# First layer's modulation on TensorE in quarters of its columns, with the norm's sums and products on VectorE

## The chip, the cores and the metric

The kernel runs on one core of a Trainium2 chip. What counts is the device time of one execution in microseconds (us). Below, a DMA is a transfer between the chip's main memory and the on-chip memory, a chunk is 128 rows of a weight matrix, and a record is one line of the profiler for one instruction on an engine.

## What is computed

Two transformer-like blocks stand one behind the other: a two-layer joint attention block with a modulation by a conditioning vector, then a block with a state-space mixer, latent attention and a gated feed-forward net. All of it is float32. The change touches the beginning of layer 0 of the first block only:

```python
silu_c = jax.nn.silu(c)            # one vector of 2048 for the 256 latent tokens
silu_cc = jax.nn.silu(c_ctx)       # one for the 256 context tokens
shift, scale, gate = jnp.split(silu_c @ w_mod[l] + b_mod[l], 3, axis=-1)
shift_c, scale_c, gate_c = jnp.split(silu_cc @ w_mod[l] + b_mod[l], 3, axis=-1)
n = rms_norm(h, pre_norm_g[l]) * (1.0 + scale[:, None]) + shift[:, None]
nc = rms_norm(hc, pre_norm_g[l]) * (1.0 + scale_c) + shift_c
p = jnp.split(n @ w_in[l], split_points, axis=-1)
```

`w_mod[0]` has 2048 rows and 6144 columns. Before the first product with `w_in` can be taken, the 4096 columns of shift and scale must have been multiplied with the two vectors.

## The kernel before

Activations lie with the 2048 features on partitions, as 16 chunks of 128 features by 512 tokens (256 latent, 256 context) in `hb`. The norm is taken in three steps: sums of squares over the features (`first_norm`, lines 824 to 843), the row `rb` of reciprocal roots (`rstd_row`), and the product of `hb` with `rb` (`times_rb`, lines 793 to 796). `norm_in` (line 784) then applies scale and shift chunk by chunk on ScalarE and splits the result into a high part `nH` and a rest `nL`.

The modulation is taken in blocks of 512 columns. `mod_first(q, steps)` (line 696) makes block q: it loads 16 chunks of 128 rows by 512 columns (`mraw`, 256 KB each), and multiplies each by the two vectors, which stand in `cs` (128 partitions, 16 chunks, 2 vectors). The odd chunks k = 1, 3, ..., 15 go to TensorE (line 708, weights `cs[:, k, :]`, two columns, output on two partitions of the PSUM bank `S`). Chunk 0 goes to ScalarE (line 706) and the even chunks 2 to 14 to VectorE (`mod_acc`, line 666), each once for either vector, into `acc`. Two more matmuls (line 717) sum `acc` over the partitions into the same bank. ScalarE copies the two rows out (line 719), and `finish`, which is run after the first chunks of the block that follows, turns them with four transposes (line 724), adds the bias (line 725), and for q below 4 makes the gains `gsc` (line 781).

The blocks come in the order 4, 0, 5, 1, 6, 2, 7, 3. Blocks 4 and 0 give scale and shift of features 0 to 511, and so on. Beside blocks 5 to 7 and 1 to 3 runs `first_steps(j)`: it takes the weights of two column groups of `w_in` for four chunks, applies `norm_in` to these four chunks, multiplies `rb` into the next four chunks on GpSimd, and issues the first products (lines 370 to 372, 96 matmuls of 256 columns for each j). It is a generator; `mod_first` advances it by one step after each chunk from the third on, which fixes the order of the instructions on each engine. The order is by hand: every engine works through its queue in program order.

The chunks land in 22 slots that go round (`slots`, 16 chunks a block), and SyncE issues each transfer when its slot has been read. The same queue carries `raw`, the weights of `w_in`.

Of the kernel before, what the change touches and what calls it, by code (L numbers as in the profile page):

```python
# [11 lines left out]
F32 = mybir.dt.float32  # L12
F32R = mybir.dt.float32r
I32 = mybir.dt.int32
AF = mybir.ActivationFunctionType
ALU = mybir.AluOpType
AX = mybir.AxisListType
ADD, SUB, MUL, MAX = ALU.add, ALU.subtract, ALU.mult, ALU.max
# [226 lines left out]
def program(ctx: ExitStack, tc: tile.TileContext, A, stop=None):  # L245
    nc = tc.nc
    V, S, P, T, SY = nc.vector, nc.scalar, nc.gpsimd, nc.tensor, nc.sync
    ctx.enter_context(tc.manual_schedule())

    const = ctx.enter_context(tc.tile_pool(name="const", bufs=1))  # L250
# [5 lines left out]
    def cst(name, shape, src=None, eng=None):  # L256
        t = const.tile(list(shape), F32, name=name)
        if src is not None:
            (eng or S).dma_start(out=t, in_=A[src])
        return t  # L260
# [3 lines left out]
    def ps_(tag):  # L264
        return psp.tile([128, 512], F32, tag=tag, name=tag, bufs=PSB[tag])
# [254 lines left out]
    ident = cst("ident", [128, 128], "ident")  # L520
# [1 line left out]
    V.memset(ones, 1.0)  # L522
    mhalf = const.tile([128, 8], F32, name="mhalf")
    V.memset(mhalf, -0.5)
    sel = const.tile([128, 2, 2], F32, name="sel")
    V.memset(sel, 0.0)
    for v in range(2):
        V.memset(sel[:, v, v:v + 1], 1.0)
    bmod = cst("bmod", [128, 2, 48], "bmod")
    preg = cst("preg", [128, 2, 16], "preg")  # L530
    postg = cst("postg", [128, 2, 16], "postg")
# [31 lines left out]
    def rstd_row(tag, accs, n, dim, out, first=0):  # L563

        tiles, t = [], 0
        while t < n:
            w = min(128, n - t) if t or not first else first
            tiles.append((t, w))
            t += w
        pst = ps_(tag)  # L570
        for i, (t, w) in enumerate(tiles):
            for j, acc in enumerate(accs):
                T.matmul(pst[:w, i:i + 1], acc[:, t:t + w], ones[:, 0:1], start=j == 0, stop=j == len(accs) - 1)
        yield
        v, r = small("rv", 4, 1), small("rr", 4, 1)
        for w in sorted({w for _, w in tiles}):
            idx = [i for i, x in enumerate(tiles) if x[1] == w]
            c = slice(idx[0], idx[-1] + 1)
            V.tensor_scalar(v[:w, c], pst[:w, c], 1.0 / dim, EPS, op0=MUL, op1=ADD)
            P.tensor_tensor(out=r[:w, c], in0=v[:w, c], in1=mhalf[:w, c], op=ALU.pow)  # L580
        yield
        psb = ps_(tag)
        for i, (t, w) in enumerate(tiles):
            T.matmul(psb[:, t:t + w], r[:w, i:i + 1].to_broadcast([w, 128]), ident[:w, :w], start=True, stop=True)
        yield
        S.copy(out=out, in_=psb[:, :n])
# [12 lines left out]
    aw = b1.enter_context(tc.tile_pool(name="aw", bufs=2))  # L599
# [10 lines left out]
    def t2k(name="t2"):  # L610
        return aw.tile([128, 512], F32, tag="t2", name=name, bufs=3)

    def p2k(name="P"):
        return aw.tile([128, 512], F32, tag="P", name=name, bufs=3)
# [38 lines left out]
    cs = const.tile([128, 16, 2], F32, name="cs")  # L653
# [5 lines left out]
    V.scalar_tensor_tensor(out=cs, in0=thv, scalar=1.0, in1=cT, op0=ADD, op1=MUL)  # L659
    V.tensor_scalar(cs, cs, 0.5, None, op0=MUL)  # L660

    def mod_acc(acc, v, k, w, first):
        if first:
            V.tensor_scalar(acc, w, cs[:, k, v:v + 1], None, op0=MUL)
        else:
            V.scalar_tensor_tensor(out=acc, in0=w, scalar=cs[:, k, v:v + 1], in1=acc, op0=MUL, op1=ADD)  # L666
# [14 lines left out]
    def mod_load(q):  # L681

        out = [next(slot) for _ in range(16)]
        k = 0
        while k < 16:
            t, j = out[k]
            n = 1
            while k + n < 16 and n < 4 and out[k + n][0] is t:
                n += 1
            SY.dma_start(out=t[:, j:j + n, :], in_=mod_src(0, q, k, n))  # L690
            k += n
        return [t[:, j, :] for t, j in out]

    fins = []

    def mod_first(q, steps):

        raw = mod_load(q)
        ps = ps_("S")
        acc = aw.tile([128, 2, 512], F32, tag=("pth", "ptl")[q // 4], name="acc", bufs=1)  # L700
        acc = [acc[:, v, :] for v in range(2)]
        on_pe = [k for k in range(1, 16) if k not in (2,4,6,8,10,12,14)]
        for k in range(16):
            if k == 0:
                for v in range(2):
                    S.activation(out=acc[v], in_=raw[0], func=AF.Copy, scale=cs[:, 0, v:v + 1])
            elif k in on_pe:
                T.matmul(ps[:2, :], cs[:, k, :], raw[k], start=(k == on_pe[0]), stop=False)
            else:
                for v in range(2):  # L710
                    mod_acc(acc[v], v, k, raw[k], False)
            if k == 2 and fins:
                fins.pop(0)()
            elif k > 2:
                next(steps, None)
        for v in range(2):
            T.matmul(ps[:2, :], sel[:, v, :], acc[v], start=False, stop=(v == 1))
        row = aw.tile([2, 512], F32, tag="sqa", name="row", bufs=1)
        S.copy(out=row, in_=ps[:2, :])

        def finish():
            pt = ps_("X")
            for j in range(4):
                T.transpose(pt[:, 2 * j:2 * j + 2], row[:, j * 128:(j + 1) * 128], ident[:2, :2])
            V.tensor_tensor(out=mod[0][:, :, 4 * q:4 * q + 4].rearrange("p v j -> p j v"),
                            in0=pt[:, :8].rearrange("p (j v) -> p j v", v=2),
                            in1=bmod[:, 0, 4 * q:4 * q + 4].unsqueeze(2).to_broadcast([128, 4, 2]), op=ADD)
            if q < 4:
                gains(0, 4 * q, 4 * q + 4)
        fins.append(finish)  # L730

    def mod_later(l, q, vs):
# [8 lines left out]
        for k in range(16):  # L741
            w = raws.pop(k)
            for v in vs:
                mod_acc(acc[v], v, k, w, k == 0)
            if k < 14:
                raws[k + 2] = load(k + 2)
            if k % 2:
                yield
                yield
# [30 lines left out]
    def gains(l, k0, k1, vs=slice(0, 2)):  # L780
        V.scalar_tensor_tensor(out=gsc[:, vs, k0:k1], in0=mod[l][:, vs, 16 + k0:16 + k1], scalar=1.0,
                               in1=preg[:, l, k0:k1].unsqueeze(1).to_broadcast([128, vs.stop - vs.start, k1 - k0]), op0=ADD, op1=MUL)

    def norm_in(k):

        t = t2k("nrm")
        for v, c in enumerate((LATC, CTXC)):
            S.activation(out=t[:, c[0]:c[1]], in_=hb[:, k, 2 + c[0]:2 + c[1]], func=AF.Identity,
                         scale=gsc[:, v, k:k + 1], bias=mod[0][:, v, k:k + 1])
        split(nH[:, k, :], nL[:, k, :], t)  # L790
# [3 lines left out]
    def times_rb(j, eng):  # L794
        for k in range(4 * j, 4 * j + 4):
            eng.tensor_tensor(out=hb[:, k, 2:514], in0=hb[:, k, 2:514], in1=rb, op=MUL)
# [4 lines left out]
    def first_steps(j):  # L801

        ws = []
        for i in DUO:
            ws.append(W.take((0,) + WIN[i][0], 256, False))
            yield
        for k in range(4):
            norm_in(4 * j + k)
            yield
        if j < 3:  # L810
            times_rb(j + 1, P)
        for _ in range(0):
            yield
        for i in range(4):
            for ps, w, prods in zip(duo_ps, ws, map(prod_of, DUO)):
                prods(ps, w[i:i + 1], N_, (FULL, FULL), 4 * j + i, KC, lambda t, k: t[:, k, :])
                for _ in range(2):
                    yield
# [5 lines left out]
    def first_norm():  # L824
        xacc, xacc2 = p2k("xacc"), p2k("xacc2")
        for k in range(16):
            xs = hb[:, k, 2:514]
            if k < 2:
                S.activation(out=(xacc, xacc2)[k], in_=xs, func=AF.Square)
            else:  # L830
                sq = t2k("sq")
                S.activation(out=sq, in_=xs, func=AF.Square)
                if k % 3 == 1:
                    P.tensor_tensor(out=xacc2, in0=xacc2, in1=sq, op=ADD)
                else:
                    V.tensor_tensor(out=xacc, in0=xacc, in1=sq, op=ADD)
            if k % 4 == 3:
                yield
        V.tensor_tensor(out=xacc, in0=xacc, in1=xacc2, op=ADD)
        yield  # L840
        yield from rstd_row("O", [xacc], 512, D, rb)
        yield
        times_rb(0, P)

    steps = first_norm()
    for _ in range(4):
# [771 lines left out]
    def mt_(name, shape, dt=F32, src=None):  # L1618
        t = m2.tile(list(shape), dt, name=name)
        if src:  # L1620
            SY.dma_start(out=t, in_=A[src])
        return t
# [686 lines left out]
    out = mt_("out", [128, 16, 256])  # L2309
# [22 lines left out]
```

## Time and profile before

| | us |
|---|---|
| median of 3 runs (3022.82 to 3035.22) | 3023.95 |
| the profiled execution | 3022.74 |
| its span, first to last instruction | 3021.0 |
| of it up to the first gains `gsc` | 64.15 |
| from there to the second, to the third, to the fourth | 34.12, 34.10, 32.61 |
| all that follows | 2856 |

The rows further down come from the page of that one execution and from questions to its trace. PE is TensorE, PEld its weight loads, DVE VectorE, ACT ScalarE, POOL GpSimd, and SPq the queue of SyncE, from which most transfers are issued. `S`, `X`, `mm` and `PT` are PSUM banks; names in the form out<-in are those of the code.

### The profile page before, as it was taken

The page shows a single profiled execution, that of the slowest core. Times are in us where ns is not written, and L with a number is a line of the kernel's source. Part 1 is how long each engine was busy: PE and PEld are TensorE (multiplying, and loading weights), DVE is VectorE, ACT ScalarE, POOL GpSimd, SP SyncE. Part 2 cuts the span into 40 slices and gives each one's busy share as a digit, 9 for nine tenths or more (in the row PEclk, how much of TensorE's full clock was granted, in tenths as well). Part 3 has the DMA queues.
Part 4 walks back from the last instruction along what each step waited for, and adds up shares of the span by engine and source line. Part 5 has one row for each costly group of instructions (what it writes and reads, how often), then busy time and mean ns, then how long its engine had stood idle before and what let it go on. Part 6 is the DMA issues. An engine that isn't in the chain of part 4 may idle for free. (4 is left out here: it accounts for less than half of the span.)

```text
span 3021.0 us, 48873 instructions
## 1 busy us (share of the span) xinstructions
PE 2823.6 (93%) x18894; PEld 2525.3 (84%) x18894; DVE 2058.2 (68%) x3801; ACT 1289.0 (43%) x2212; POOL 553.2 (18%) x521
## 2 busy tenths in 40 slices
PE   5999999999899987999998998799899999999998
PEld 1477897897787887889898897776899999999998
DVE  6668767678677568776667887776865555455644
ACT  3335423434344344544435644234354444344443
POOL 4001100100112143010001125654531110001100
PEclk9999999999999998999999998899999999999999
DMA  8744454454445664634443464341455565665554
GB/s 306 271 129 132 129 151 129 150 155 139 118 122 157 209 188 160 199 118 139 149 142 100 145 215 140 124 128 61 145 166 176 183 182 183 185 186 184 185 175 154
DMA packets 176441, 483.96 MB, mean 160 GB/s; under 512 B 20944, under 2 KB 32848, under 8 KB 176208
## 3 DMA queue, kind: packets, MB, share of 16 engines
q1 hardware_dynamic: 171312, 468.62, 49.9%
q0 software_dynamic: 2880, 9.96, 0.9%
q8 instruction: 148, 2.42, 0.3%
q10 hardware_dynamic: 2016, 2.25, 0.2%
q14 instruction: 85, 0.70, 0.1%
HBM read 468.71 MB, written 12.06 MB: 159 GB/s over the span
## 5 line engine op out<-in xcount | busy, mean ns | idle before, releaser
L327 DVE TENSOR_TENSOR wl<-raw,wh 128x1024 fp32r<-128x1024 f32 (+2 forms) x650 | 813.5, 1256 | 441.0 <-ACT wh L313 436.3
L313 ACT CAST wh<-raw 128x1024 fp32r<-128x1024 f32 (+2 forms) x650 | 669.7, 1036 | 924.2 <-PE mm L465 571.5
L464 PE MATMUL mm<-nH,wh 128*128 128x512 f32 (+1 forms) x2048 | 705.2, 344 | 11.8 <-ACT kp L1121 6.7
L465 PE MATMUL mm<-nL,wh 128*128 128x512 f32 (+1 forms) x2048 | 697.7, 341 | 4.6 <-DVE nL L1109 4.6
L466 PE MATMUL mm<-nH,wl 128*128 128x512 f32 (+1 forms) x2048 | 696.9, 340 | 3.5 <-DVE wl L327 3.5
L464 PEld LDWEIGHTS mm<-nH,wh 128*128 128x128 f32 x2048 | 390.3, 191 | 63.8 <-ACT kp L1121 7.1
L666 DVE SCALAR_TENSOR_TENSOR acc<-mraw,cs,acc 128x512 f32<-128x512 f32 x532 | 383.5, 775 | 80.9 <-DMA mraw<-in_wmod 46.2
L465 PEld LDWEIGHTS mm<-nL,wh 128*128 128x128 f32 x2048 | 390.2, 191 | 51.1 <-DVE nL L1109 6.4
L466 PEld LDWEIGHTS mm<-nH,wl 128*128 128x128 f32 x2048 | 389.4, 190 | 51.3 <-DVE wl L327 4.3
L464 PE MATMUL mm<-ZA,wh 128*128 128x258 f32 (+1 forms) x1408 | 400.4, 284 | 5.0 <-DVE oa L1910 5.0
L466 PE MATMUL mm<-ZA,wl 128*128 128x258 f32 (+1 forms) x1408 | 399.9, 284 | 0.0
L465 PE MATMUL mm<-ZB,wh 128*128 128x258 f32 (+1 forms) x1290 | 363.9, 282 | 0.0
L464 PEld LDWEIGHTS mm<-ZA,wh 128*128 128x128 f32 x1408 | 267.3, 190 | 5.2 <-issue 5.2
L466 PEld LDWEIGHTS mm<-ZA,wl 128*128 128x128 f32 x1408 | 267.5, 190 | 0.0
L465 PEld LDWEIGHTS mm<-ZB,wh 128*128 128x128 f32 x1290 | 245.3, 190 | 0.0
L370 PE MATMUL mm<-wh,nH 128*128 128x256 f32 x736 | 212.9, 289 | 8.9 <-ACT nH L470 4.7
L372 PE MATMUL mm<-wh,nL 128*128 128x256 f32 x736 | 210.8, 286 | 5.3 <-DVE nL L471 3.8
L371 PE MATMUL mm<-wl,nH 128*128 128x256 f32 x736 | 209.8, 285 | 0.0
L464 PE MATMUL mm<-yH,wh 128*128 128x256 f32 x688 | 193.3, 281 | 0.0
L465 PE MATMUL mm<-yL,wh 128*128 128x256 f32 x688 | 193.3, 281 | 0.0
L466 PE MATMUL mm<-yH,wl 128*128 128x256 f32 x688 | 193.3, 281 | 0.0
L370 PEld LDWEIGHTS mm<-wh,nH 128*128 128x128 f32 x736 | 141.2, 192 | 30.6 <-issue 18.1
(502 smaller groups left out, 4846.1 us busy)
## 6 DMA issues: line engine op xcount, KB each, us to landing
raw<-in_win SPq DMA_DIRECT2D x266, 512.0 KB, 3.8
raw<-in_wup SPq DMA_DIRECT2D x172, 512.0 KB, 4.2
mraw<-in_wmod SPq DMA_DIRECT2D x288, 256.0 KB, 2.9
raw<-in_wout SPq DMA_DIRECT2D x76, 512.0 KB, 4.0
raw<-in_wda SPq DMA_DIRECT2D x40, 512.0 KB, 3.6
raw<-in_wdb SPq DMA_DIRECT2D x40, 512.0 KB, 4.3
mraw<-in_wmod SPq DMA_DIRECT2D x28, 512.0 KB, 5.4
mraw<-in_wmod SPq DMA_DIRECT2D x10, 1024.0 KB, 5.7
```

Source lines behind the costliest of these rows:

```text
L313: S.copy(out=h[:, :size], in_=self.raw[j][:, :size])
L327: V.tensor_sub(lo[:, :size], r[:, :size], h[:, :size].bitcast(F32))
L370: T.matmul(o, ah, w[i][0], start=(k == 0 and t % 2 == 0), stop=False)
L371: T.matmul(o, ah, w[i][1], start=False, stop=False)
L372: T.matmul(o, al, w[i][0], start=False, stop=(k == nk - 1 and t % 2 == 1 and last and i == len(w) - 1))
L464: T.matmul(out, wh, ah, start=start, stop=False)
L465: T.matmul(out, wh, al, start=False, stop=False)
L466: T.matmul(out, wl, ah, start=False, stop=stop)
L666: V.scalar_tensor_tensor(out=acc, in0=w, scalar=cs[:, k, v:v + 1], in1=acc, op0=MUL, op1=ADD)
```

## The change

The sums of all 16 chunks of a block go to TensorE. The two columns of `cs` are padded with 30 columns of zeros to 32 (`csq`), and of each four chunks the first writes partitions 0 to 31 of the bank `S`, the second 32 to 63, and so on: four matmuls in a row on four quarters of the array's columns. A block then leaves four partial sums for either vector; ScalarE copies all 128 partitions, and in `finish` four matmuls with a selector `sel` of two columns sum the quarters and turn the result at once, in place of the four transposes. The products of ScalarE and VectorE with the chunks and the two matmuls with `acc` are gone. `first_steps` is advanced by two steps after the first four chunks of a block, and by four after each further four. All sums of squares, a third of which were on GpSimd, and the products with `rb` go to VectorE.

```diff
-    sel = const.tile([128, 2, 2], F32, name="sel")
-    V.memset(sel, 0.0)
-    for v in range(2):
-        V.memset(sel[:, v, v:v + 1], 1.0)
+
+    sel = const.tile([128, 2], F32, name="sel")
+    V.tensor_reduce(out=sel, in_=ident.rearrange("p (j c) -> p c j", c=32)[:, 0:2, :], axis=AX.X, op=ADD)
...
+    csq = aw.tile([128, 16, 32], F32, tag="pth", name="csq", bufs=1)
+    V.memset(csq, 0.0)
+    V.tensor_copy(out=csq[:, :, 0:2], in_=cs)
...
         ps = ps_("S")
-        acc = aw.tile([128, 2, 512], F32, tag=("pth", "ptl")[q // 4], name="acc", bufs=1)
-        acc = [acc[:, v, :] for v in range(2)]
-        on_pe = [k for k in range(1, 16) if k not in (2,4,6,8,10,12,14)]
-        for k in range(16):
-            if k == 0:
-                for v in range(2):
-                    S.activation(out=acc[v], in_=raw[0], func=AF.Copy, scale=cs[:, 0, v:v + 1])
-            elif k in on_pe:
-                T.matmul(ps[:2, :], cs[:, k, :], raw[k], start=(k == on_pe[0]), stop=False)
-            else:
-                for v in range(2):
-                    mod_acc(acc[v], v, k, raw[k], False)
-            if k == 2 and fins:
+        for k0 in range(0, 16, 4):
+
+            for j in range(4):
+                T.matmul(ps[32 * j:32 * j + 32, :], csq[:, k0 + j, :], raw[k0 + j], start=(k0 == 0), stop=(k0 == 12))
+            if k0 == 0 and fins:
                 fins.pop(0)()
-            elif k > 2:
+            for _ in range(2 if k0 == 0 else 4):
                 next(steps, None)
-        for v in range(2):
-            T.matmul(ps[:2, :], sel[:, v, :], acc[v], start=False, stop=(v == 1))
-        row = aw.tile([2, 512], F32, tag="sqa", name="row", bufs=1)
-        S.copy(out=row, in_=ps[:2, :])
+        row = aw.tile([128, 512], F32, tag=("sqa", "ptl")[q // 4], name="row", bufs=1)
+        S.copy(out=row, in_=ps)
...
-                T.transpose(pt[:, 2 * j:2 * j + 2], row[:, j * 128:(j + 1) * 128], ident[:2, :2])
+                T.matmul(pt[:, 2 * j:2 * j + 2], row[:, j * 128:(j + 1) * 128], sel, start=True, stop=True)
...
-            times_rb(j + 1, P)
-        for _ in range(0):
-            yield
+            times_rb(j + 1, V)
...
-                if k % 3 == 1:
-                    P.tensor_tensor(out=xacc2, in0=xacc2, in1=sq, op=ADD)
-                else:
-                    V.tensor_tensor(out=xacc, in0=xacc, in1=sq, op=ADD)
+                V.tensor_tensor(out=(xacc, xacc2)[k % 2], in0=(xacc, xacc2)[k % 2], in1=sq, op=ADD)
...
-        times_rb(0, P)
+        times_rb(0, V)
```

On TensorE, at the start of the program, from the first chunk of block 4 to the first products of `first_steps(0)`. `S<-mraw` are the modulation's matmuls (x4: four in a row), `O` the norm's sum and its spreading, `X` the turn in `finish`. Before:

```order
L708 MATMUL S<-mraw,cs 2x512 x2
L573 MATMUL O<-ones,xacc 128x1 x4
L708 MATMUL S<-mraw,cs 2x512
L584 MATMUL O<-ident,rr 128x128 x4
L708 MATMUL S<-mraw,cs 2x512 x5
L717 MATMUL S<-acc,sel 2x512 x2
L708 MATMUL S<-mraw,cs 2x512
L724 MATMUL X<-ident,row 128x2 x4
L708 MATMUL S<-mraw,cs 2x512 x7
L717 MATMUL S<-acc,sel 2x512 x2
L708 MATMUL S<-mraw,cs 2x512
L724 MATMUL X<-ident,row 128x2 x4
```

With the change, for the same stretch:

```order
L706 MATMUL S<-mraw,csq 32x512 x4
L572 MATMUL O<-ones,xacc 128x1 x4
L706 MATMUL S<-mraw,csq 32x512 x4
L583 MATMUL O<-ident,rr 128x128 x4
L706 MATMUL S<-mraw,csq 32x512 x12
L717 MATMUL X<-sel,row 128x2 x4
L706 MATMUL S<-mraw,csq 32x512 x16
L717 MATMUL X<-sel,row 128x2 x4
L706 MATMUL S<-mraw,csq 32x512 x8
```

Behind the spreading of the norm now stand 28 modulation matmuls up to the second turn, where 18 stood; none of them waits for `acc`, and before the first product of `w_in` come eight more instead of four.

On VectorE, from the turn of block 0 to that of block 5, beside `first_steps(0)`. `wl` is the rest of a weight, `nL` that of a normed chunk. Before:

```order
L725 TENSOR_TENSOR mod_90<-X,bmod 128x4x2
L666 SCALAR_TENSOR_TENSOR acc<-mraw,cs,acc 128x512 x14
L725 TENSOR_TENSOR mod_90<-X,bmod 128x4x2
L781 SCALAR_TENSOR_TENSOR gsc<-mod_90,preg 128x2x4
L327 TENSOR_TENSOR wl<-raw,wh 128x1024
L666 SCALAR_TENSOR_TENSOR acc<-mraw,cs,acc 128x512 x2
L327 TENSOR_TENSOR wl<-raw,wh 128x1024
L471 TENSOR_TENSOR nL<-nrm,nH 128x512
L666 SCALAR_TENSOR_TENSOR acc<-mraw,cs,acc 128x512 x2
L471 TENSOR_TENSOR nL<-nrm,nH 128x512 x2
L666 SCALAR_TENSOR_TENSOR acc<-mraw,cs,acc 128x512 x2
L471 TENSOR_TENSOR nL<-nrm,nH 128x512
```

With the change:

```order
L789 TENSOR_TENSOR hb<-hb,rb 128x512 x4
L718 TENSOR_TENSOR mod_88<-X,bmod 128x4x2 x2
L774 SCALAR_TENSOR_TENSOR gsc<-mod_88,preg 128x2x4
L327 TENSOR_TENSOR wl<-raw,wh 128x1024 x2
L471 TENSOR_TENSOR nL<-nrm,nH 128x512 x4
L789 TENSOR_TENSOR hb<-hb,rb 128x512 x4
```

The products with the chunks are gone from the queue, and four products with `rb` stand ahead of the first turn and four behind each set of `nL`. The queue of SyncE keeps its order.

## Rows read from the trace of the kernel before

**Rows 1.** The page: busy us of each engine, share of the span, instructions.

```profile
PE 2823.6 (93%) x18894; PEld 2525.3 (84%) x18894; DVE 2058.2 (68%) x3801; ACT 1289.0 (43%) x2212; POOL 553.2 (18%) x521
```

**Rows 2.** Busy us by stretch: PE, PEld, DVE, ACT, POOL; then granted clock, DMA share, GB/s.

```profile
21.30:64.15 42.85, 29.33 (x68) 7.83 (x69) 32.98 (x37) 7.24 (x12) 26.97 (x18) 0.84 0.86 314
64.15:98.27 34.12, 32.99 (x147) 15.34 (x146) 23.72 (x40) 11.98 (x21) 0.00 (x0) 1.00 0.82 280
```

**Rows 3.** Timeline (start us, us): VectorE makes the gains of four chunks.

```profile
64.15 0.15 DVE L781 SCALAR_TENSOR_TENSOR gsc<-mod,preg 128x8 f32<-128x8 f32 x1
98.27 0.15 DVE L781 SCALAR_TENSOR_TENSOR gsc<-mod,preg 128x8 f32<-128x8 f32 x1
132.37 0.15 DVE L781 SCALAR_TENSOR_TENSOR gsc<-mod,preg 128x8 f32<-128x8 f32 x1
164.98 0.16 DVE L781 SCALAR_TENSOR_TENSOR gsc<-mod,preg 128x8 f32<-128x8 f32 x1
```

**Rows 4.** Timeline of the first stretch, all engines; in brackets idle time and releaser.

```profile
31.92 4.78 PE L708 MATMUL S<-mraw,cs 128*2 128x512 f32 x10
32.69 23.89 POOL L796 TENSOR_TENSOR hb<-hb,rb 128x512 f32<-128x512 f32 x16 [2.83 <-ACT rb L586]
39.54 6.17 PE L708 MATMUL S<-mraw,cs 128*2 128x512 f32 x14
42.14 16.31 DVE L666 SCALAR_TENSOR_TENSOR acc<-mraw,cs,acc 128x512 f32<-128x512 f32 x12
57.84 3.57 PE L717 MATMUL S<-acc,sel 128*2 128x512 f32 x4 [12.13 <-DVE acc L666]
```

**Rows 5.** Groups by line up to 175 us: busy us, mean ns, idle before, releasers.

```profile
L708 PE MATMUL S<-mraw,cs 128*2 128x512 f32 x128 | 64.8, 623 | 21.3 <-DMA mraw<-in_wmod 21.3
L666 DVE SCALAR_TENSOR_TENSOR acc<-mraw,cs,acc 128x512 f32<-128x512 f32 x112 | 85.7, 829 | 33.7 <-ACT acc L706 33.7
L471 DVE TENSOR_TENSOR nL<-nrm,nH 128x512 fp32r<-128x512 f32 x16 | 10.7, 687 | 3.1 <-ACT nH L470 3.1
```

**Rows 6.** Transfers: bytes moved up to 46.5 us, and two stretches as in rows 2.

```profile
DMA packets 9292, 16.17 MB, mean 348 GB/s; under 512 B 1608, under 2 KB 1992, under 8 KB 9292
9.00:50.00 41.00, 23.03 (x56) 6.67 (x56) 30.29 (x37) 13.76 (x24) 25.29 (x17) 1.00 1.04 384
50.00:64.15 14.15, 6.30 (x12) 1.19 (x13) 9.86 (x10) 2.64 (x4) 6.58 (x5) 0.53 0.50 164
```

**Rows 7.** Timeline of PE where it goes from products to modulation and back.

```profile
72.39 0.28 PE L372 MATMUL PT<-wh,nL 128*128 128x256 f32 x1
72.60 1.02 PE L708 MATMUL S<-mraw,cs 128*2 128x512 f32 x2
73.56 0.38 PE L370 MATMUL mm<-wh,nH 128*128 128x256 f32 x1
73.78 0.28 PE L371 MATMUL mm<-wl,nH 128*128 128x256 f32 x1
73.89 0.28 PE L372 MATMUL mm<-wh,nL 128*128 128x256 f32 x1
```

**Rows 8.** Timeline of PE: a later turn by matmuls, and the next matmul's start.

```profile
322.11 0.95 PE L770 MATMUL X<-half,acc 128*128 128x2 f32 x8
322.92 0.47 PE L464 MATMUL mm<-nH,wh 128*128 128x512 f32 x1
```

**Rows 9.** Timeline of PE: six matmuls on halves of the rows, between whole ones.

```profile
240.98 0.98 PE L1276 MATMUL S<-qkk,qkq 64*128 64x512 f32 x6
241.89 0.50 PE L464 MATMUL mm<-nH,wh 128*128 128x512 f32 x1
242.23 0.40 PE L465 MATMUL mm<-nL,wh 128*128 128x512 f32 x1
242.46 0.40 PE L466 MATMUL mm<-nH,wl 128*128 128x512 f32 x1
```

**Rows 10.** Timeline of ScalarE: the norm of one chunk.

```profile
65.11 1.09 ACT L788 ACTIVATE nrm<-hb,mod,gsc 128x256 f32<-128x256 f32 x2
66.23 0.62 ACT L470 CAST nH<-nrm 128x512 fp32r<-128x512 f32 x1
```

## The prediction, made before the changed kernel ran

> **What bounds the kernel now.** I began with the busy times: TensorE is busy 93% of the span [rows 1], so elsewhere nothing but TensorE's own work counts. The chain of waits does not reach back to the stage that the change touches, so I read that stage by its milestones. The gains of the four groups of chunks are made at 64.15, 98.27, 132.37 and 164.98 us [rows 3]; the stage is one stretch up to the first gains and three periods of 34.12, 34.10 and 32.61 us. The instructions after the fourth gains keep their kinds and their order; what is won or lost before should be kept to the end, unchanged.
>
> The *first stretch* is bound by VectorE and by what GpSimd does to it. TensorE stands idle for 12.13 us until VectorE has finished `acc` of block 0 [rows 4]. VectorE takes 16.31 us for 12 products there, 1.36 us each, while GpSimd multiplies `rb` into `hb` for 23.89 us [rows 4]; the mean over the stage is 0.83 us [rows 5]. So the first stretch is late because VectorE is slowed beside GpSimd, and all of that goes with the change.
>
> The *periods* are bound by TensorE: 32.99 of 34.12 us busy, transfers at 280 GB/s, where 384 were reached while they were full [rows 2, 6]. The 64 modulation matmuls of line 708 leave 128 records [rows 5]: each float32 matmul goes through the array as two records, one behind the other. Fourteen records take 6.17 us from the first start to the last end [rows 4]; with 0.59 us for the last to drain (1.02 us for two records less one step [rows 7]) a step is (6.17 - 0.59)/13 = 0.43 us, a matmul 0.86 us. A product with `w_in` takes 0.12 us a step [rows 7]. Going from products to modulation and back costs 0.09 us at the first border (0.21 from L372 to L708 instead of 0.12), 0.10 at the second (0.96 for two records instead of 0.86) and 0.10 for the first product's successor (0.22 instead of 0.12): 0.29 us for the round trip [rows 7]. A period then is 20 matmuls x 0.86 = 17.2, 96 products x 0.12 = 11.5, eight or nine round trips 2.5, two turns 0.7, and some 2 us in which the products wait for the norm: 33.9, and 34.1 was measured. The account closes.
>
> **The change, part by part.** The question that decides is how long a matmul on a quarter of the columns takes when its neighbours use the other quarters. No row of before shows that. The nearest one is that of six matmuls on halves of the rows [rows 9]: from their first start to the next whole matmul pass 0.91 us; whole ones of the same 512 columns step by 0.23 us (242.23 to 242.46), so six in a row would take 1.4 us, while three steps plus the border's 0.2 give 0.9. Two parts of the array do work side by side. For quarters of columns I assume the same, with one limit: of the two records of one matmul the second uses the same quarter as the first, and records have started in program order wherever I looked. So in the sequence A1 A2 B1 B2 C1 C2 D1 D2 only A2 and B1, B2 and C1, C2 and D1 can overlap. A run of n matmuls then takes n + 1 steps of 0.43 us instead of 2n: **two abreast, not four**.
>
> The second unknown is the weight load. From a border to the second product, the load of 128 columns shows as 0.10 us [rows 7]; inside a run it is hidden. If it is hidden between quarters, it costs nothing; if each matmul shows its load of 32 columns, a quarter of that, 0.03 us, 32 times in a period, 0.9 us. I take half. The Trainium skill, "TensorE: Matmul & The Clock Gate", Part 3 ("The mechanism"), says that weight loads overlap with matmuls in flight only where the row group differs, which speaks against this change, since quarters of columns share all rows; by it the sum has the full 0.9 us a period.
>
> *Periods.* On TensorE there are now 32 modulation matmuls, in runs of 8, 4, 4, 4, 4 and 8 between the products: 38 steps x 0.43 = 16.3 us (17.2 before). Products 11.5. Five round trips 1.45. Two turns: eight records of a turn by matmuls take 0.81 us from 322.11 to 322.92 [rows 8], 1.6 for both. Weight loads 0.45. Sum 31.3 us. The norm of the first chunk after the gains takes 1.09 + 0.62 us on ScalarE [rows 10] and 0.69 on VectorE [rows 5]; two `wl` stand ahead of it there. It is covered by the run of eight, some 3.9 us, that now stands between the gains and the first product; the wait of 2 us goes. So a period is 2.8 us shorter, twice. The last one lacks the next block's first four matmuls (1.7 us) but waits 0.9 us for ScalarE's copy and the turn: 30.5 instead of 32.6, 2.1 less. *Transfers*: a period moves 32 chunks and two units of `w_in`, 9.4 MB, 24.6 us at 384 GB/s [rows 6]; they stay hidden.
>
> *First stretch.* Bound from TensorE: the work behind the norm starts at 31.92 [rows 4]; 28 matmuls in runs of 12 and 16 are 30 steps, 12.9 us, and two turns 1.6: 46.4. Bound from transfers: the first four chunks of block 5, ahead of the turn of block 0, are complete when 16.2 MB have come (norm input 4.2, constants 1.0, blocks 4 and 0 8.4, `w_in` 1.0, six chunks 1.6). The queue's order is unchanged and the engines were full up to 50 us, so that is at 46.5 us as in before [rows 6]. Then two matmuls 1.3, the turn 0.8, the bias and the gains 0.5: **49.1 us** instead of 64.15, 15 less. The granted clock was 0.84 in this stretch, since the half level (1.2 GHz) followed TensorE's idle time [rows 2, 6]; here TensorE's idle time would be a few us at most, and its work has a little room beneath the transfers.
>
> *VectorE, ScalarE, GpSimd.* Four products with `rb` at 0.69 (the row of `nL`, the same shape [rows 5]) are 2.8 us a period, in place of 28 products with a mean of 0.83; between 0 and 1.5 us each if GpSimd's speed is the bound (23.89/16 [rows 4]), at most 6 us in a period where VectorE now has over 20 free. Queued behind them is only the bias of the next turn. The four more sums of squares are 2.8 us beside the arriving input. All of this is hidden.
>
> Sum: -15 - 2.8 - 2.8 - 2.1 = -22.7 us, against the profiled execution's own 3022.74: **3000 us**. That execution lies 1.2 us below the median of the three runs, well within their spread. With weight loads at either end, 0 and twice 0.9, and the first gains between 46 and 52 us, the case reaches from 2994 to 3009.
>
> **The rivals.** *Serial*: the quarters do not overlap for float32, and each matmul takes 0.86 us as before. Then the first stretch ends at 31.92 + 28 x 0.86 + 1.6 + 0.5 = 58 us (-6). A period has 27.5 + 11.5 + 1.45 + 1.6 = 42.0 us (+7.9, twice), the last 42.0 - 3.4 + 0.9 = 39.5 (+6.9). Together +16.7: **3039 us**, slower. For it: half the chunks were on other engines, and this moves them onto the engine that bounds the periods. Against it: rows 9. It decides from about 0.65 us a matmul on: each 0.1 above 0.43 costs 3.2 us a period.
>
> *Four abreast*: eight records of a run of four take two steps. Then modulation is 6.9 us a period, TensorE's sum 21.5, and transfers become the bound with 24.6 a period: -9.5, -9.5, -8, and -16 in the first stretch, **2980 us**. For it: nothing in the rows excludes it. Against it: it asks that a second record lets another matmul's first one pass. The Trainium skill, "TensorEngine Tiling (Array Packing)", "Theoretical Speedup", gives up to four times for at most 32 columns; by that the time is this rival's. Rows 9 bear it out for two parts, not for four.
>
> *Slots late*: two abreast, but a four needs all its four chunks and so waits for the slowest of several transfers; a group of four that waits 0.5 us in each of 24 groups costs 12 us: **3012 us**. For it: transfers ran at 280 of 384 GB/s already [rows 2, 6], and rise to 305. Against it: 22 slots run more than a block ahead.
>
> **How the numbers follow.** Two abreast 0.60, four abreast 0.12, slots late 0.13, serial 0.15. Forecast 3000 us. The range leaves out the serial case: 2978 to 3014. About 0.5%, or 15 us, is what a measurement of this kernel can tell from no change. Faster by more: nearly all of the first case, all of the second, a third of the third, 0.75. Within: the rest of the third and half of the serial one, 0.16. Slower: 0.09.
>
> **What would show it.** The first gains at about 49 us, and no wait of TensorE for `acc`; the further ones at intervals of 31.3, 31.3 and 30.5. The start-to-start time of modulation records decides: alternately 0.43 us and nearly nothing if two go abreast, 0.43 throughout if serial. Transfers in the periods should rise from 280 to about 305 GB/s. GpSimd's busy time should fall by over 24 us, VectorE's by some 70. I am wrong if the intervals stay near 34 (weight loads or slots), grow to 42 (serial), or if the time after the fourth gains is not the 2856 us of before.

## The result, and the profile after

| | before, us | after, us |
|---|---|---|
| median | 3023.43 | 2982.84 |
| lowest to highest of 4 | 3022.82 to 3035.22 | 2980.39 to 2983.73 |
| the profiled execution | 3022.74 | 2980.39 |
| first gains | 64.15 | 51.51 |
| the three intervals that follow | 34.12, 34.10, 32.61 | 23.62, 24.08, 23.17 |
| all behind the fourth gains | 2856.0 | 2856.2 |

The changed kernel is faster: 0.9855 of the time before, 95% interval 0.983 to 0.988. The forecast was 3000, the time 2983; it lies in the range, but the gain, 40.6 us by the medians, is nearly twice the 22.7 us of the forecast, and it is that of the rival *four abreast* (2980).

The page of after, in the form of [rows 1]; below it VectorE's gains, as in [rows 3]:

```profile
PE 2798.6 (94%) x19022; PEld 2530.3 (85%) x19022; DVE 1980.7 (66%) x3709; ACT 1279.2 (43%) x2196; POOL 526.1 (18%) x501
```

```profile
51.51 0.16 DVE L774 SCALAR_TENSOR_TENSOR gsc<-mod,preg 128x8 f32<-128x8 f32 x1
75.13 0.16 DVE L774 SCALAR_TENSOR_TENSOR gsc<-mod,preg 128x8 f32<-128x8 f32 x1
99.21 0.16 DVE L774 SCALAR_TENSOR_TENSOR gsc<-mod,preg 128x8 f32<-128x8 f32 x1
122.38 0.16 DVE L774 SCALAR_TENSOR_TENSOR gsc<-mod,preg 128x8 f32<-128x8 f32 x1
```

TensorE's busy share hardly moves. The milestones tell where the time went: 12.6 us in the first stretch, then 10.5, 10.0 and 9.4, together 42.6; the profiled executions differ by 42.4. Nothing of it is given back later.

Stretches of after, with the columns of [rows 2] (busy us of PE, PEld, DVE, ACT, POOL; granted clock, DMA share, GB/s): the first stretch, the three intervals, the rest.

```profile
21.30:51.50 30.20, 23.32 (x108) 7.42 (x108) 4.84 (x11) 3.95 (x6) 1.02 (x1) 0.88 1.05 389
51.51:75.13 23.62, 23.62 (x180) 15.24 (x179) 7.81 (x15) 8.97 (x16) 0.00 (x0) 0.94 1.04 387
75.13:99.21 24.08, 23.06 (x180) 15.22 (x176) 7.76 (x14) 9.57 (x17) 0.00 (x0) 1.00 1.05 389
99.21:122.38 23.17, 22.20 (x168) 14.98 (x160) 7.78 (x14) 9.36 (x17) 0.00 (x0) 1.00 0.78 294
122.40:2978.60 2856.20, 2705.89 (x18398) 2477.25 (x18398) 1943.71 (x3642) 1237.54 (x2126) 524.86 (x496) 0.97 0.50 154
```

Before, the transfers ran at 280 GB/s in an interval [rows 2]; now they run at 387 and 389 in the first two, near the 384 that were reached before only up to 50 us [rows 6]. In these two intervals TensorE (23.62 of 23.62 us busy, at a granted clock of 0.94, and 23.06 of 24.08) and the transfers are at or near their limit at the same time.

How a run of four goes is seen on PE between two products, the place of [rows 7]:

```profile
57.62 0.28 PE L372 MATMUL PT<-wh,nL 128*128 128x256 f32 x1
57.83 1.06 PE L706 MATMUL S<-mraw,csq 128*32 128x512 f32 x8
58.83 0.39 PE L370 MATMUL mm<-wh,nH 128*128 128x256 f32 x1
```

Four matmuls leave eight records, and from the start of the first to the next product pass 1.00 us. In [rows 7] one matmul took 0.96 us from its start to the next product. So three more cost 0.04 us. Singly the eight records start at 57.832, 57.838, 57.844 and 57.852, then the second four between 58.284 and 58.305: all four first records within 20 ns, all four second ones a step of 0.45 us later. The first four alone (window 57.83 to 57.86) last 0.64 us; one behind the other, at steps of 0.43, it would be 1.9:

```profile
57.83 0.64 PE L706 MATMUL S<-mraw,csq 128*32 128x512 f32 x4
```

In the first stretch TensorE no longer waits for `acc`, as it did in [rows 4], but for transfers:

```profile
45.05 1.92 PE L706 MATMUL S<-mraw,csq 128*32 128x512 f32 x4 [2.96 <-DMA mraw<-in_wmod]
47.68 1.92 PE L706 MATMUL S<-mraw,csq 128*32 128x512 f32 x4 [0.71 <-DMA mraw<-in_wmod]
49.52 1.87 PE L717 MATMUL X<-sel,row 128*128 128x2 f32 x8
```

### The profile page after: what moved, and what is told of

Its sections match the earlier page's. It is cut to its first block, busy times and chain, and to the rows that moved or that the text cites. A ratio compares the mean times of both kernels' runs of the same rounds, so it can differ in the third digit from the quotient of the medians.

```text
span 2978.6 us, 48955 instructions
## 1 busy us (share of the span) xinstructions
PE 2798.6 (94%) x19022; PEld 2530.3 (85%) x19022; DVE 1980.7 (66%) x3709; ACT 1279.2 (43%) x2196; POOL 526.1 (18%) x501
## 5 line engine op out<-in xcount | busy, mean ns | idle before, releaser
L669 DVE SCALAR_TENSOR_TENSOR acc<-mraw,cs,acc 128x512 f32<-128x512 f32 x420 | 295.6, 754 | 45.8 <-DMA mraw<-in_wmod 43.8
L2258 POOL TENSOR_TENSOR v<-v,a 128x256 f32<-128x256 f32 x43 | 59.4, 1381 | 562.8 <-ACT a L2257 549.6
```

The costliest lines, as they stand in the source:

```text
L2258: P.tensor_tensor(out=v, in0=v, in1=a, op=MUL)
```

## The experiments

Theory A, formed from these rows: matmuls on different quarters start together, whatever stands between them in the program. Rival B: the matmuls still go one or two at a time, and the gain came from the other engines, the waits for `acc` or the norm. Behind both stands a further question: what bounds the stage now. All times are medians; ratios are against the kernel before, run beside it. Runs of one kernel spread by 3 to 19 us, mostly behind the stage (in single executions the time behind the fourth gains went from 2854 to 2868 us for the same instructions), so what happens in the stage is read from the milestones.

**All on one quarter.** After, but every matmul of a four writes the same 32 partitions.

```diff
-                T.matmul(ps[32 * j:32 * j + 32, :], csq[:, k0 + j, :], raw[k0 + j], start=(k0 == 0), stop=(k0 == 12))
+                c = 32 * (0)
+                T.matmul(ps[c:c + 32, :], csq[:, k0 + j, :], raw[k0 + j], start=(k0 == 0 and j == 0), stop=(k0 == 12 and j == 3))
```

> The changed kernel, but all chunks of a block go to the first quarter of the columns (output on partitions 0 to 31), so that no two modulation matmuls can go side by side; all that was taken from VectorE, ScalarE and GpSimd stays away from them. Theory A (four quarters at once are the gain, and with them the transfers became the bound): each matmul takes two steps of 0.43 us, the intervals of the gains grow to about 42 us, 3039 us in all. Rival B (the gain comes from the freed VectorE and GpSimd, the packing is little): the time stays within 10 us of the changed kernel's 2983.

Measured: 3043.47 us, 1.0069 [1.0052, 1.0086], slower than before. The gains come at 57.91, 100.49, 143.07 and 182.95 us, intervals of 42.58, 42.58 and 39.88. A run of four on PE, and the second gains:

```profile
67.78 3.62 PE L707 MATMUL S<-mraw,csq 128*32 128x512 f32 x8
100.49 0.16 DVE L775 SCALAR_TENSOR_TENSOR gsc<-mod,preg 128x8 f32<-128x8 f32 x1
```

The matmuls and the relief of the other engines are those of after, and the whole gain is gone. (Not in the lines shown: ScalarE's copy and the turn take only the 32 partitions that are written, in the two runs that follow 64.) The eight records take 3.62 us in place of 1.06. The first gains still come 6.2 us earlier than before, without the wait for `acc`; the intervals are 7.3 to 8.5 us longer than before and use that up. So the gain on the whole needs the quarters.

**Two quarters, in turn** (A B A B): the same edit with `c = 32 * (j % 2)`.

> The changed kernel with two quarters in use instead of four, taken in turn (A B A B). Theory A, with records that start as soon as their quarter is free: four matmuls take four steps, 1.7 us and the border; a period is 13.8 + 11.5 + 1.45 + 2.0 = 28.7 us, and the whole 2997 us. If records start in program order only (the limit that my forecast set): five steps for four matmuls, 2.15 us, periods of 31, 3001 us or more. Rival B: 2983.

**Two quarters, one behind the other** (A A B B): `c = 32 * (j // 2)`. In program order the first two matmuls use the same quarter. If the order of starts were that of the program, the second matmul on A would hold back the first on B.

> Two quarters again, but two matmuls behind each other on the same quarter (A A B B). If a record may start ahead of records that stand before it in the program and wait for their own quarter, this is as fast as the order in turn: 1.7 us for four, 2997 us. If records start in program order, only the last of A goes beside the first of B: seven steps, 3.0 us for four, periods of about 38, 3024 us.

Measured: 2999.18 us, 0.9923 [0.9903, 0.9943], in turn; 3003.95, 0.9932 [0.9911, 0.9952], one behind the other. The two are not told apart by these times, though 3003.95 is 7 us above the 2997 expected: in its profiled execution 2867.9 us stand behind the fourth gains, in that of the other 2854.0. A run of four in either, the first row in turn, the second one behind the other:

```profile
60.26 1.91 PE L707 MATMUL S<-mraw,csq 128*32 128x512 f32 x8
```

```profile
61.75 1.92 PE L707 MATMUL S<-mraw,csq 128*32 128x512 f32 x8
```

Four steps of 0.43 us with the last one's drain, in both. Strict program order in A A B B would be seven steps for the eight records, over 3 us. The single records show the first on A at 61.751 and the first on B at 61.765 us: the third matmul of the program starts 14 ns after the first and ahead of the second. These two alone (window 61.755 to 61.77):

```profile
61.75 0.63 PE L707 MATMUL S<-mraw,csq 128*32 128x512 f32 x2
```

That the second of them is the third matmul is seen from its weight load, which waits for the semaphore of the transfer that brings the third chunk. One behind the other the load with this wait starts second in the run, at 61.763; for the same run in turn, where the third matmul uses A again, it starts at 65.623, 0.46 us behind the first. The intervals agree: 28.99, 28.96 and 28.03 us one behind the other, 31.82, 28.88 and 27.95 in turn. The 31.82 goes with a granted clock of 0.91 in that interval, against 1.00 in the others (9% of it are 2.9 us, as much as it lies above 28.88):

```profile
50.90:82.72 31.82, 31.82 (x178) 17.28 (x176) 7.80 (x15) 9.61 (x16) 0.00 (x0) 0.91 0.99 360
82.72:111.60 28.88, 28.88 (x178) 16.88 (x176) 7.76 (x14) 9.61 (x16) 0.00 (x0) 1.00 0.92 327
```

So the records of a quarter waited for one another here, and not for earlier records of another quarter. One, two and four quarters give intervals of 42.6, 28.9 and 23.6 to 24.1 us. From one to two the 32 matmuls give 13.7 us, 16 times 0.86; from two to four only 5, where halving the matmuls again would give 8 times 0.86, 6.9. The next run asks why.

**Half of the chunks loaded.** After, with 8 chunks a block, each used twice. It leaves half of the modulation's sum out, and half of its transfers.

```diff
-        out = [next(slot) for _ in range(16)]
+        out = [next(slot) for _ in range(8)]
...
-        return [t[:, j, :] for t, j in out]
+        return [out[k // 2][0][:, out[k // 2][1], :] for k in range(16)]
```

> The changed kernel, but a block loads 8 chunks instead of 16 and uses each for two matmuls; it leaves out half of the modulation's sum (each loaded chunk counts twice). All instructions of the engines are the same, the stage moves 16.8 MB less. If transfers bound the stage (theory A): the first gains come some 13 us earlier, at about 38 us, and the intervals fall to TensorE's own 21.5 to 22 us; about 2964 us. If TensorE or another engine bounds it: 2983.

Measured: 2968.23 us, 0.982 [0.9791, 0.9849]. The first gains come at 37.27 instead of 51.51, so the first stretch is bound by transfers. The intervals are 23.24, 23.21 and 23.13, not the 21.5 to 22 expected. The first gains, and the second interval:

```profile
37.27 0.16 DVE L774 SCALAR_TENSOR_TENSOR gsc<-mod,preg 128x8 f32<-128x8 f32 x1
```

```profile
60.51:83.72 23.21, 22.37 (x180) 15.16 (x176) 7.77 (x15) 9.43 (x17) 0.00 (x0) 1.00 0.62 227
```

With the transfers at 227 GB/s, far from full, an interval still takes 23.2: this is TensorE's own period, 0.84 us of it idle. From two quarters to four that is 5.7 us, and the idle time, which the interval of 28.88 us does not have, is most of what is missing to 6.9. Full loads cost 0.9 us more in the second interval, where TensorE waits 1.0 us for a transfer, and nothing in the third (23.17). The 0.4 of the first come without such a wait, at a granted clock of 0.94. The two bounds lie nearly on each other.

**The norm alone.** Before, with only the norm's sums and products moved from GpSimd to VectorE; the modulation stays as it was.

```diff
-            times_rb(j + 1, P)
+            times_rb(j + 1, V)
...
-                if k % 3 == 1:
-                    P.tensor_tensor(out=xacc2, in0=xacc2, in1=sq, op=ADD)
-                else:
-                    V.tensor_tensor(out=xacc, in0=xacc, in1=sq, op=ADD)
+                V.tensor_tensor(out=(xacc, xacc2)[k % 2], in0=(xacc, xacc2)[k % 2], in1=sq, op=ADD)
...
-        times_rb(0, P)
+        times_rb(0, V)
```

> The kernel before with one part of the change: the sums of squares and the products with rb on VectorE, the modulation as it was. If GpSimd's products were what slowed VectorE (1.36 us a product beside them, 0.67 to 0.71 without), VectorE gets the first stretch done earlier although it has 20 more instructions there in all: first gains at 55 to 58 us instead of 64.15, the intervals as before at 34, about 3016 us. If GpSimd did not slow it, VectorE has 5 to 10 us more work in the first stretch: gains at 68 or later, 3027 us.

Measured over 12 executions: 3021.5 us, 0.9984 [0.9973, 0.9996], 1 to 8 us less than the kernel before beside it (3026.49). The first gains come at 53.73 instead of 64.15, still earlier than expected, and VectorE shows why:

```profile
53.73 0.16 DVE L781 SCALAR_TENSOR_TENSOR gsc<-mod,preg 128x8 f32<-128x8 f32 x1
40.69 8.03 DVE L666 SCALAR_TENSOR_TENSOR acc<-mraw,cs,acc 128x512 f32<-128x512 f32 x12
```

The same 12 products took 16.31 us beside GpSimd [rows 4]. The intervals then are 35.49, 35.17 and 33.67, not as before, as was expected, but each over 1 us longer; VectorE has four products with `rb` more there beside its chunks, and in the first interval TensorE waits 1.0 us for `acc`, as it did not before. Of 10.4 us in the first stretch 6.9 are left at the fourth gains.

**The quarters without the norm's move.** After, with these lines as they were before, on GpSimd.

> The changed kernel with the other part alone: modulation on four quarters, while the norm's sums (a third of them) and products are on GpSimd as before. Theory A (transfers bound the stage): VectorE has nothing to lose, the first gains come at 51 to 52 us and the intervals stay at 23 to 24, within 3 us of 2983. If the move of the norm was needed for the gain: the first gains come later by 4 us or more, 2987 us or more.

Measured: 2982.19 us, 0.9862 [0.9843, 0.9881], gains at 51.28, 75.26, 99.22 and 122.39: those of after, within 0.3 us. GpSimd multiplies `rb` into `hb` for 16.83 us and nobody is late for it:

```profile
51.28 0.17 DVE L774 SCALAR_TENSOR_TENSOR gsc<-mod,preg 128x8 f32<-128x8 f32 x1
122.39 0.16 DVE L774 SCALAR_TENSOR_TENSOR gsc<-mod,preg 128x8 f32<-128x8 f32 x1
```

```profile
28.68 16.83 POOL L789 TENSOR_TENSOR hb<-hb,rb 128x512 f32<-128x512 f32 x16 [1.91 <-ACT rb L585]
```

The norm's move and the quarters both take away the same wait, that for a slow `acc`. Once the quarters have, the move is worth nothing.

**Tables later.** After, with three tables that are not needed before the attention (0.79 MB) loaded behind the weights of the stage.

```diff
-    S.dma_start(out=rope, in_=A["rope"])
-    S.dma_start(out=win, in_=A["win"])
-    S.dma_start(out=nam, in_=A["na"])
...
+    SY.dma_start(out=rope, in_=A["rope"])
+    SY.dma_start(out=win, in_=A["win"])
+    SY.dma_start(out=nam, in_=A["na"])
```

> The changed kernel, but the three tables that no instruction of this stage reads (rope, win, nam, 0.79 MB) are loaded behind the stage's last weights instead of ahead of the first. If transfers bound the stage from its start, the first gains come 0.79 MB / 388 GB/s = 2.0 us earlier, at 49.5 us, with the same intervals, and the whole takes some 2 us less than the changed kernel; if not, nothing moves.

**And the turn ahead of the block's first four.** In addition `finish` is run ahead of the next block's first four matmuls, not behind them.

> The kernel with the three tables late, and the turn of a block ahead of the first four matmuls of the next block instead of behind them, so that the gains no longer wait for the next block's first chunks. The first gains then come with block 0 alone, at about 42 us instead of 49.3. If the periods are bound by TensorE's own 23.2 us, all later gains move along by 7 us and the whole takes 2972 us. If the last transfers set the end (they stop at about 115.5 us), the intervals grow and the fourth gains come at 118 to 119 us instead of 120.3: 2977 us.

**After once more**, unaltered, beside the two runs on the norm and the one on the tables.

> The changed kernel again, unaltered, on the same chip as the three others: 2983 us, first gains at 51.5 us.

Measured: 2979.15 us, 0.9851 [0.9832, 0.9869], for the tables; 2981.3, 0.9851 [0.9835, 0.9867], with the turn moved too; 2981.75, 0.9854 [0.9838, 0.987], unaltered. By these times none is told from after. The milestones can: with the tables later the first gains come at 49.28 and the fourth at 120.28, 2.2 and 2.1 us earlier than in after:

```profile
49.28 0.17 DVE L771 SCALAR_TENSOR_TENSOR gsc<-mod,preg 128x8 f32<-128x8 f32 x1
120.28 0.15 DVE L771 SCALAR_TENSOR_TENSOR gsc<-mod,preg 128x8 f32<-128x8 f32 x1
```

With the turn moved the first come at 41.78, but the intervals grow to 30.06, 25.40 and 23.07, and the fourth stand at 120.31:

```profile
41.78 0.17 DVE L771 SCALAR_TENSOR_TENSOR gsc<-mod,preg 128x8 f32<-128x8 f32 x1
120.31 0.16 DVE L771 SCALAR_TENSOR_TENSOR gsc<-mod,preg 128x8 f32<-128x8 f32 x1
```

```profile
41.78:71.84 30.06, 25.72 (x180) 16.15 (x184) 7.81 (x15) 9.54 (x17) 0.00 (x0) 0.89 1.05 388
71.84:97.24 25.40, 23.02 (x180) 15.16 (x176) 7.77 (x15) 9.52 (x17) 0.00 (x0) 1.00 1.05 389
50.00:113.00 63.00, 59.84 (x464) 40.73 (x459) 17.90 (x31) 19.53 (x33) 0.00 (x0) 0.99 1.05 389
```

7.5 us won on TensorE at the start are all given back, while the transfers run at 388 to 389 GB/s. TensorE waits 3.7 us for them in the first interval, where its granted clock is also 0.89, and 1.6 us in the second, at the full clock. The end of the stage is then set by the bytes; of what was tried with the whole modulation kept, only fewer bytes ahead of it, as with the tables, moved it. Neither number of the expectation came: the fourth gains do not move to 118 or 119 us but stay where the tables alone had put them.

## Why the prediction was right and wrong

**The step that failed** is "of the two records of one matmul the second uses the same quarter as the first, and records have started in program order wherever I looked", from which "two abreast, not four" followed. Its first half holds. The second was read where it could not show: in [rows 7] all records use the whole array, so none could pass another. The rows on halves [rows 9] showed that parts work side by side, not in what order: the two halves take turns in the program (line 1276), so strict order would have held none of them back. A A B B at 14 ns between the starts shows that the order of the program does not hold across quarters; the sentence ahead of the prediction that every engine works through its queue in program order is too wide there. The Trainium skill, "TensorE: Matmul & The Clock Gate", Part 3 ("The mechanism"), says that matmuls start and end strictly in order; the starts of A A B B speak against that here. Its "TensorEngine Tiling (Array Packing)", "Theoretical Speedup", gives up to four times for at most 32 columns; four matmuls in 1.00 us instead of the 3.55 on one quarter (67.78 to the next product at 71.33) agree, with 3.6.

**The arithmetic was sound in the main.** Two quarters in turn are nearly what the sum described (four steps for four matmuls where it put five), and they give 2999 us; the serial rival was put at 42.0 us an interval and 3039, and 42.6 and 3043 were measured, its profiled execution at 3039.05. What was wrong was which of the cases the chip is in: 0.60 went to two abreast and 0.12 to four. Some of the agreement is luck. Two quarters at the full clock have intervals of 28.9 us and not 31.3; the first gains 1.8 us later than forecast and the low clock of one interval take most of that back. The rival's 2980 puts the first stretch 3.4 us too early and its three intervals 2.9 us too long in all, which cancel. The range held 2983 only because it was drawn down to 2978 to take this rival in. The reach of the main case, 2994 to 3009, is a slip: its own terms give 2996 to 3007.

**The weight load** was given half of 0.9 us a period. It is nearly nothing. In a run of four the second records start 0.45 us after the first, 0.02 more than a step. On one quarter that excess stands once in a run too (67.776 to 68.230, then steps of 0.43), so six runs a period have 0.15 us of it; whether it is the load is not shown. All other 32-column loads stand inside the steps. The group of weight loads of line 706 up to 130 us (count, busy, mean ns, idle before):

```profile
L706 PEld LDWEIGHTS S<-mraw,csq 128*32 128x32 f32 x256 | 7.5, 113 | 46.8 <-DVE xacc L824 20.8 <-DMA mraw<-in_wmod 16.5 <-issue 7.3
```

The sentence of the Trainium skill, "TensorE: Matmul & The Clock Gate", Part 3 ("The mechanism"), that weight loads overlap only where the row group differs is not borne out: all four quarters share their rows, and the loads are hidden with a single quarter in use as well.

**The periods**, if the rival's case is taken: its TensorE sum was 21.5 us, its transfers 24.6, so 24.6. Measured 23.6 and 24.1. The transfers were sized rightly to 1 us. TensorE's sum fell short by 1.7: a period with half the loads is 23.2. Of that, 0.84 is idle time, all of it for the norm (0.5 us for `nH`, 0.3 for `nL`), which the forecast had covered by eight matmuls of 3.9 us and which four abreast cover with 1.9; two turns took 0.3 more. The rest, some 0.6 with the 0.15 above, I did not place.

**The first stretch** was put at 49.1 and measured 51.51, the one stretch that gained less than forecast. The bound was named rightly, the first four chunks of block 5. They are complete at 47.68 instead of 46.5. By then 16.74 MB have come, half a megabyte more than the 16.2 of the account (transfers up to 47.7 us):

```profile
DMA packets 9605, 16.74 MB, mean 351 GB/s; under 512 B 1643, under 2 KB 2027, under 8 KB 9605
```

And behind them 3.8 us pass up to the gains, not 2.6, since the clock is at the lower level (1.2 GHz):

```profile
42.00:47.68 5.68, 2.01 (x7) 0.22 (x5) 0.00 (x0) 2.49 (x3) 0.00 (x0) 0.70 1.04 387
47.68:55.00 7.32, 7.32 (x30) 2.80 (x31) 3.15 (x5) 3.17 (x6) 0.00 (x0) 0.53 1.05 386
```

TensorE was busy for 2.01 of 5.68 us ahead of it, waiting for transfers, and then worked at a granted clock of 0.53: the turn's eight records took 1.80 us from start to start (49.52 to 51.32), which later take 0.91 to 0.99, and the two matmuls ahead of it 1.92 us, which ten microseconds earlier took 1.05:

```profile
36.97 1.05 PE L706 MATMUL S<-mraw,csq 128*32 128x512 f32 x4 [0.29 <-DMA mraw<-in_wmod]
```

"TensorE's idle time would be a few us at most" was true (3.67 us in these 5.68), and the clock fell all the same.

**What held.** No wait of TensorE for `acc`; GpSimd's busy time 27 us less (24 forecast at least), VectorE's 77.5 (70); the rest 2856 us, unchanged. The new work on VectorE is hidden, at the duration forecast:

```profile
L789 DVE TENSOR_TENSOR hb<-hb,rb 128x512 f32<-128x512 f32 x16 | 10.0, 686 | 3.0 <-ACT rb L585 3.0
```

The reason given for the first stretch, VectorE slowed by GpSimd, was right for the kernel before: 16.31 us against 8.03 without it. That it "goes with the change" was right too, but for the reason that the products go; the norm's half of the change has no part in it.

*Slots late* did not come about: the transfers run full, and the waits for `mraw` that remain are the transfers' own pace. The four abreast were the case for which the forecast had said that "nothing in the rows excludes it", and the chance given to it was too small for that.

## What to carry to other kernels

When small matmuls with at most 32 output columns share a stage with large ones, spread them over the four column quarters in groups of four. Here four then cost 1.00 us where one had cost 0.96. The next bound has to be sought at once: here the transfers, with TensorE's own period less than 1 us below them. Where a kernel's rows cannot show the order of two things because they always shared a resource, that order is unknown and both cases deserve a like chance. And of two edits that remove the same wait, measure each alone before giving either a price of its own.

## What the runs showed of the hardware

- Float32 matmuls leave two records each, and a record waited for those of its own quarter, not for earlier ones of another: four first records start within 20 ns, ahead of second records that precede them in the program; in A A B B the first on B starts 14 ns after the first on A.
- Weight loads of 32 columns, 0.113 us each in the mean, are hidden beside matmuls on the same rows, on other quarters (four matmuls in 1.00 us) and on their own (steps of 0.43 us on one quarter); of their time at most 0.02 us a run of four shows.
- VectorE's products of 128x512 took 0.67 us each with GpSimd at rest and 1.36 beside GpSimd's products, 8.03 against 16.31 us for 12. GpSimd's own took 1.49 us beside them (23.89 for 16) and 1.05 when VectorE had none (16.83 for 16): both are slowed.
- One core took in 386 GB/s over 108 us, from 9 to 117 us (after).
